# Four small moves in a TensorE-bound encoder layer: places for evacuated tiles, a logarithm in more steps, a later refill, a half-row store

## Chip, core and metric

One core of a Trainium2 chip runs the whole program. The metric is device time in microseconds (us), the median of several executions. TensorE (PE) multiplies, VectorE (DVE) and ScalarE (ACT) work element by element, GpSimd (POOL) does small work beside them, and SyncE (SP) issues the DMA transfers. All five run their own instruction stream in the order in which it was compiled.

## The reference

A hybrid encoder layer with three head groups runs over two request groups of 1024 and 256 rows, with weights in common; the kernel treats their 1280 rows as two halves of 640. All is float32.

```python
def layer(x, mem, ...):
    hn = rms_norm(x, norm_g)
    proj = hn @ w_in                       # 2048 -> xbc, z_ssd, dt, q, k, v, z_att, mq, z_mem
    xbc = silu(centred_dwconv(xbc, ...))
    dt = softplus(dt_raw + dt_bias)
    y = ssd_scan(forward) + ssd_scan(backward) + d_skip * xs      # decay = exp(cumsum(dt * A)), x * dt
    o_ssd = rms_norm(y * silu(z_ssd), ssd_norm_g)
    o_att = window_attention(q, k, v, sink) * silu(z_att)
    o_mem = softmax(mq @ mk.T) @ mv * silu(z_mem)
    return x + concat([o_ssd, o_att, o_mem]) @ w_out
```

## The kernel before

**Products.** Every float32 operand of the large products is split into a high part that TensorE takes in one pass and a low part (the rest), and each product is three matmuls, high by high, low by high, high by low. Weights arrive in pieces of 128x512 (`wraw`, four buffers) and are split by `wsplit` (L214 to L218): ACT copies the high part (`wh`, L216), DVE subtracts for the low part (`wl`, L217). The other operand lies split in SBUF in four quads, `xH0` to `xH3` and `xL0` to `xL3`.

**Blocks.** The program is a list of blocks. `block_tok` (L244) makes 640 rows by 512 columns in five sums (`acc`), one for each 128 rows, over 16 k-steps; the last two k-steps are done tile by tile, so that the five sums end one after the other, and each is evacuated while the next one runs. `block_feat` (L278) is the same with the result turned, and `block_pair` (L1287) makes a product in seven sums instead of eight. The first half's projections come first, then from 493 us on the second half's: kv, z1 of the first half, x0 to x5, kv, q, za, z0, z1, mq, zm, and then the output product o0 to o3 for the first half, and eight `block_pair` units for the second. Blocks follow each other on PE without a gap, and an evacuated tile (`qs` of `ev_raw`, L335; `zs` of `ev_gate`, L315) goes to DRAM from one of two tags, `evt` and `evu`, with two buffers each.

**Beside the blocks.** Everything else (attention, memory attention, the scan) is written as generators in two lanes. `pump` (L158) takes so many steps of each lane for a k-step; a `yield` is where a step ends, and `need` (L169) runs lanes until a given generator is done. A scheduler then orders each engine's stream by its own estimate of the times, so an instruction may be compiled well ahead of or behind its place in the code; on the chip the stream is fixed.

**What the change touches.** `dt_prep` (L568) makes the step sizes for five tiles of 128 rows: a softplus on DVE, `da` (L593), the logarithm's first guess (L596, L597), the sums over rows on PE (`pacs`, L608 to L610, which read `da`, and `lower`, a triangle made on POOL), and two rounds that sharpen the logarithm. A round is an exponential on ACT (L614, `s`) and five operations on DVE (L616 to L620), and the next round's exponential needs the last of them. `refill_o` (L1531) loads the first half's finished heads from DRAM (`oT`) through `chd` (tag `ch`, four buffers) and splits them into a quad; its table says at which k-step which quad is started. `ev_pair` (L1232) adds the seven sums of an output unit into two rows of 640 and stores them. The streams that matter are ACT's, in which a waiting instruction holds the `wh` behind it, and SP's, in which a waiting transfer holds the `wraw` loads behind it.

Of the kernel before, what the change touches and what calls it, by code (L numbers as in the profile page):

```python
# [44 lines left out]
def hymba_encoder_kernel(  # L45
# [80 lines left out]
    def hv(ap, n=8):  # L126
        return ap.rearrange("p (h d) -> p h d", h=n)
# [184 lines left out]
            evac(1, ps[1])  # L312


    def ev_gate(c, base):  # L315
        def f(i, ps):
            z = ev.tile([P, 512], F32, tag="evt" if i % 2 else "evu", name="zs")
            A.activation(z, ps, AF.Tanh, scale=0.5)
            V.scalar_tensor_tensor(out=z, in0=z, scalar=1.0, in1=ps, op0=ALU.add, op1=ALU.mult)
            S.dma_start(z_d[c][base + i], z)  # L320
        return f
# [12 lines left out]

    def ev_raw(dst, base):  # L335
        def f(i, ps):
            if base == 0 and i > 2:
                z = fin.tile([P, 512], F32, tag="tH7" if i == 4 else "tL7", name="qs")
            else:
                z = ev.tile([P, 512], F32, tag="evt" if i % 2 else "evu", name="qs")  # L340
            last_raw[0] = A.activation(z, ps, AF.Copy).ins
            S.dma_start(dst[base + i], z)
        return f
# [224 lines left out]
    def dt_prep(t0):  # L568
        grp = t0 // 5
        ts = slice(t0, t0 + 5)  # L570
        flat = lambda a: a[:, ts, :].rearrange("p t h -> p (t h)")
        t6 = (t0 + 1) % 6
        wj, dd = [a[:, t6:t6 + 5, :].rearrange("p t h -> p (t h)") for a in (wj_all, dd_all)]
        t5 = lambda a: a.rearrange("p (t h) -> p t h", t=5)
        x = flat(dt_all)
        e, s = [mp.tile([P, 512], F32, tag="xs", name=n, bufs=2)[:, :160] for n in "es"]
        w, l = [mp.tile([P, 512], F32, tag=f"ya{i}", name=n, bufs=1)[:, :160] for i, n in enumerate("wl")]
        V.scalar_tensor_tensor(out=e, in0=x, scalar=-1.0, in1=x, op0=ALU.mult, op1=ALU.min)
        A.activation(e, e, AF.Exp)
        V.tensor_scalar(out=s, in0=e, scalar1=2.0, scalar2=None, op0=ALU.add)  # L580
        V.reciprocal(out=s, in_=s)
        V.tensor_mul(s, s, e)
        V.tensor_mul(w, s, s)
        V.tensor_scalar(out=e, in0=w, scalar1=1.0 / 17, scalar2=None, op0=ALU.mult)
        for c in (15, 13, 11, 9, 7, 5, 3):
            V.scalar_tensor_tensor(out=e, in0=e, scalar=1.0 / c, in1=w, op0=ALU.add, op1=ALU.mult)
        V.scalar_tensor_tensor(out=e, in0=e, scalar=1.0, in1=s, op0=ALU.add, op1=ALU.mult)
        V.tensor_scalar(out=e, in0=e, scalar1=2.0, scalar2=None, op0=ALU.mult)
        V.scalar_tensor_tensor(out=x, in0=x, scalar=0.0, in1=e, op0=ALU.max, op1=ALU.add)
        yield  # L590

        da = e
        V.tensor_mul(t5(da), dt_all[:, ts, :], aneg.unsqueeze(1).broadcast_to([P, 5, 32]))  # L593
        yield

        V.tensor_scalar(out=w, in0=x, scalar1=1e-30, scalar2=None, op0=ALU.max)  # L596
        V.tensor_scalar(out=l, in0=w.bitcast(I32), scalar1=math.log(2.0) / 2 ** 23, scalar2=-126.957 * math.log(2.0),  # L597
                        op0=ALU.mult, op1=ALU.add)
        yield
        yield  # L600
        lower = w2("lower")[:, :P]
        G.affine_select(out=lower, in_=ones, compare_op=ALU.is_ge, fill=0.0, base=0,
                        pattern=[[-1, P]], channel_multiplier=1)
        yield
        yield
        ps = psum("pacs")
        p5 = t5(ps[:, :160])
        T.matmul(p5[:, :, 0:16], upper, t5(da)[:, :, 0:16], start=True, stop=True)  # L608
        T.matmul(p5[:, :, 16:32], lower, t5(da)[:, :, 16:32], start=True, stop=True)
        T.matmul(ps[:, 160:320], ones, da, start=True, stop=True)  # L610
        ac = wb("ac", shape=(P, 512))
        A.activation(ac[:, :320], ps[:, :320], AF.Copy)
        for _ in range(2):
            A.activation(s, l, AF.Exp)  # L614
            d = da
            V.tensor_sub(d, w, s)  # L616
            V.tensor_add(s, w, s)
            V.reciprocal(out=s, in_=s)
            V.tensor_mul(d, d, s)
            V.scalar_tensor_tensor(out=l, in0=d, scalar=2.0, in1=l, op0=ALU.mult, op1=ALU.add)  # L620
        A.activation(flat(eacs_all), ac[:, 0:160], AF.Exp)
        A.activation(flat(cd_all), ac[:, 160:320], AF.Exp)
        V.tensor_sub(wj, l, ac[:, 0:160])
        V.tensor_add(dd, wj, ac[:, 160:320])
        A.activation(dd, dd, AF.Exp)
        V.tensor_sub(t5(wj)[:, :, 16:32], t5(wj)[:, :, 16:32], t5(wj)[:, :, 0:16])
        yield
        ps = psum("pact")
        T.transpose(ps[:, :P], ac[:, 0:128], ident)
        T.transpose(ps[:32, P:2 * P], ac[:, 128:160], ident)  # L630
        acT = wb("acT", shape=(P, 512))
        A.activation(acT[:, :P], ps[:, :P], AF.Copy)
        A.activation(acT[:32, P:2 * P], ps[:32, P:2 * P], AF.Copy)
        S.dma_start(ac_d[grp][0:P, :], acT[:, :P])
        S.dma_start(ac_d[grp][P:160, :], acT[:32, P:2 * P])
        yield
# [595 lines left out]
    def ev_pair(u):  # L1232
# [9 lines left out]
        def f(p, ps):  # L1242
            if p == 1:
                A.activation(w[:, 0], ps, AF.Copy)
                add(r0[:, 0], ps, r0[:, 0])
            elif p == 2:
                add(r0[:, 0], ps, r0[:, 0])
            elif p == 6:
                add(w[:, 0], ps, w[:, 0])
            elif p == 5:  # L1250
                add(w[:, 1], ps, w[:, 0])
                add(r0[:, 1], w[:, 1], r0[:, 1])
                add(r1, w, r1)
            elif p == 3:
                add(r0[:, 1], ps, r0[:, 1])
                S.dma_start(hv(y_turned[rows_[0], :], 2), r0)
            elif p == 7:
                add(r1, ps.unsqueeze(1).broadcast_to([P, 2, 320]), r1)
                S.dma_start(y_turned[rows_[1], 320:], r1[:, 1])
            else:  # L1260
                add(r1[:, 0], ps, r1[:, 0])
                S.dma_start(y_turned[rows_[1], :320], r1[:, 0])
# [265 lines left out]
                         gain=vec[:, R_G + 4 * q + j:R_G + 4 * q + j + 1], norm=True) for j in range(4)]  # L1528
        return f

    def refill_o(grp, when):  # L1531
        def f(k):
            if k not in when:
                return []
            q = when[k]
            need((attn, mem_attn, ssd_down, ssd_down)[q], range(grp * 5, grp * 5 + 5))
            return [part(fill_direct, q, j, oT_d[q][grp][:, j, :],
                         gain=None if q < 2 else vec[:, R_SG + 4 * (q - 2) + j:R_SG + 4 * (q - 2) + j + 1])
                    for j in range(4)]
# [171 lines left out]
    queue(0, mem_values, [1])  # L1711
    queue(0, mem_attn, range(8, 10))
    for c in range(2):
        tok("o", w_out_rows(c), ev_out(c * 512), None if c else refill_o(0, {1: 2, 5: 3}), grp=1)
    for c in range(2, 4):
        j0 = 16 * (c - 3)
        for k in block_tok(w_out_rows(c), 5, ev_out(c * 512), before_last=lambda _: beside_step(j0 + 14)):
# [91 lines left out]
```

## Time and profile before

| what | us |
|---|---|
| median of 3 executions (1772.21 to 1774.35) | 1772.34 |
| the profiled execution | 1773.66 |
| its span, first to last instruction | 1772.0 |
| PE busy in it | 1762.2 |
| DVE, ACT, POOL busy | 1246.0, 901.6, 555.6 |

The profile was taken of one execution, whose own time was 1.32 us over the median. Lines of the form "start, length, engine, line, operation, out<-in" are single instructions, or runs of equal ones with their count; what stands in brackets is how long the engine sat idle just before, and which event ended that. The end of a matmul is modelled: a 128x512 one is shown as 0.39 us long, and the next one starts 0.23 us after it. The granted clock of TensorE is a share of its full speed.

### The profile page before, as it was taken

To read this page: it belongs to the slowest core of one execution; us is meant where nothing else is said; L and a number is where in the kernel's file an instruction comes from. 1 tells how busy PE (TensorE), PEld (TensorE's weight loads), DVE (VectorE), ACT (ScalarE), POOL (GpSimd) and SP (SyncE) were. 2 spreads that over 40 slices of the span, in tenths; PEclk is the share of its full clock that TensorE was granted. 3 is DMA by queue.
4 is the path that set the end of the run, shared out by engine and by line. 5 is a ranking of instruction groups with operands and counts; after the bars stand their busy time and mean duration, and the time that the engine had idled before them with its cause. 6 is when DMAs were issued, how large, how long until landed. Compare 5 with 4: busy or idle time off the path is not lost. (4 is left out here: it accounts for less than half of the span.)

```text
span 1772.0 us, 31942 instructions
## 1 busy us (share of the span) xinstructions
PE 1762.2 (99%) x11044; PEld 1608.4 (91%) x11044; DVE 1246.0 (70%) x2351; ACT 901.6 (51%) x2010; POOL 555.6 (31%) x980
## 2 busy tenths in 40 slices
PE   9999999999999999999999999999999999999999
PEld 7889999999998999999889988888988888899999
DVE  5596788888868878878665676566776654766665
ACT  6555455554434756656454555544446533543332
POOL 0105899998810100001001000011110000058775
PEclk9999999999999999999999999999999999999999
DMA  9654444445446645454545645557777755744442
GB/s 308 189 182 130 136 151 146 144 140 169 124 140 209 197 134 151 140 153 122 186 121 173 201 149 161 172 161 249 225 246 226 257 188 148 218 142 148 145 144 77
DMA packets 208210, 301.16 MB, mean 170 GB/s; under 512 B 19568, under 2 KB 86192, under 8 KB 208048
## 3 DMA queue, kind: packets, MB, share of 16 engines
q1 hardware_dynamic: 207904, 299.06, 54.1%
q8 instruction: 87, 1.43, 0.3%
q14 instruction: 75, 0.61, 0.1%
q10 hardware_dynamic: 144, 0.06, 0.0%
HBM read 236.36 MB, written 62.69 MB: 169 GB/s over the span
## 5 line engine op out<-in xcount | busy, mean ns | idle before, releaser
L217 DVE TENSOR_TENSOR wl<-wraw,wh 128x512 fp32r<-128x512 f32 (+1 forms) x480 | 346.4, 724 | 238.4 <-ACT wh L216 225.4
L216 ACT ACTIVATE wh<-wraw 128x512 fp32r<-128x512 f32 (+1 forms) x480 | 292.2, 613 | 301.6 <-PE acc L270 154.6
L268 PE MATMUL acc<-wh,xH 128*128 128x512 f32 (+1 forms) x1088 | 418.1, 385 | 0.0
L270 PE MATMUL acc<-wh,xL 128*128 128x512 f32 (+1 forms) x1088 | 410.4, 377 | 0.0
L269 PE MATMUL acc<-wl,xH 128*128 128x512 f32 (+1 forms) x1088 | 409.5, 376 | 0.0
L270 PEld LDWEIGHTS acc<-wh,xL 128*128 128x128 f32 x1088 | 204.2, 188 | 37.0 <-issue 0.2
L268 PEld LDWEIGHTS acc<-wh,xH 128*128 128x128 f32 x1088 | 204.3, 188 | 36.5 <-issue 2.7
L269 PEld LDWEIGHTS acc<-wl,xH 128*128 128x128 f32 x1088 | 204.5, 188 | 35.0 <-issue 1.2
L303 PE MATMUL acc<-xH,wh 128*128 128x320 f32 x640 | 203.0, 317 | 0.0
L305 PE MATMUL acc<-xH,wl 128*128 128x320 f32 x640 | 198.8, 311 | 0.0
L304 PE MATMUL acc<-xL,wh 128*128 128x320 f32 x640 | 198.5, 310 | 0.0
L216 ACT ACTIVATE sh<-ws 128x384 fp32r<-128x384 f32 x176 | 91.4, 523 | 204.8 <-POOL ws L1284 111.2
L217 DVE TENSOR_TENSOR sl<-ws,sh 128x384 fp32r<-128x384 f32 x176 | 124.4, 710 | 98.3 <-ACT sh L216 96.0
L1284 POOL TENSOR_TENSOR ws<-wraw 128x128 f32<-128x128 f32 x176 | 113.8, 646 | 202.4 <-DMA wraw<-in_w_in_pairs_dram 90.5
L303 PEld LDWEIGHTS acc<-xH,wh 128*128 128x128 f32 x640 | 120.1, 188 | 2.9 <-issue 2.4
L304 PEld LDWEIGHTS acc<-xL,wh 128*128 128x128 f32 x640 | 120.2, 188 | 1.7 <-issue 1.4
L305 PEld LDWEIGHTS acc<-xH,wl 128*128 128x128 f32 x640 | 120.2, 188 | 1.0 <-issue 0.9
L1284 POOL TENSOR_TENSOR ws<-wraw,ws 128x128 f32<-128x128 f32 x176 | 116.5, 662 | 13.8
L1284 POOL TENSOR_TENSOR ws<-ws,wraw 128x128 f32<-128x128 f32 x176 | 118.2, 671 | 0.0
L1284 POOL TENSOR_TENSOR wraw<-wraw 128x128 f32<-128x128 f32 x176 | 111.5, 633 | 13.7
L654 POOL MEMSET lgw<- 128x1 f32 x40 | 4.2, 105 | 312.0 <-DVE lg L718 161.6
L377 DVE SCALAR_TENSOR_TENSOR c<-u,vec,c 128x638 f32<-128x638 f32 (+1 forms) x96 | 90.0, 939 | 1.1 <-ACT c L372 0.4
(442 smaller groups left out, 3931.1 us busy)
## 6 DMA issues: line engine op xcount, KB each, us to landing
wraw<-in_w_in_laid_dram SPq DMA_DIRECT2D x176, 256.0 KB, 2.9
wraw<-in_w_in_pairs_dram SPq DMA_DIRECT2D x112, 256.0 KB, 2.7
wraw<-in_w_out_laid_dram SPq DMA_DIRECT2D x64, 256.0 KB, 3.6
wraw<-in_w_out_pairs_dram SPq DMA_DIRECT2D x64, 256.0 KB, 2.7
rf<-ac SPq DMA_DIRECT2D x40, 256.0 KB, 4.0
rb<-ac SPq DMA_DIRECT2D x40, 256.0 KB, 4.7
wraw<-in_w_mem_laid_dram SPq DMA_DIRECT2D x32, 256.0 KB, 4.3
xst<-in_x_sample_dram SPq DMA_DIRECT2D x20, 256.0 KB, 5.3
```

The source lines that it names most:

```text
L216: a = A.activation(h, raw, AF.Copy)
L217: b = V.tensor_sub(l, raw, h.bitcast(F32))
L268: T.matmul(ps[t][:, :n], sh, h[:, :n], start=(k_ == 0), stop=False)
L269: T.matmul(ps[t][:, :n], sh, l[:, :n], start=False, stop=False)
L270: T.matmul(ps[t][:, :n], sl, h[:, :n], start=False, stop=(k_ == KT - 1))
L303: T.matmul(o, sh, cur["H", q][:, m, c], start=(k == 0), stop=False)
L304: T.matmul(o, sh, cur["L", q][:, m, c], start=False, stop=False)
L305: T.matmul(o, sl, cur["H", q][:, m, c], start=False, stop=(k == KT - 1))
L377: V.scalar_tensor_tensor(out=c[0], in0=u[:, k:k + n], scalar=cw[k], in1=c[0], op0=ALU.mult, op1=ALU.add)
L654: G.memset(w.bitcast(F32)[(slice(None),) + tuple(slice(n - 1, n) for n in shape)], 0.0)
L1284: G.tensor_tensor(out=o, in0=x, in1=y, op=op)
```

## The change

Five edits, none of which changes a product.

1. `out_place` gives the place of an evacuated tile. In the second half's `ev_raw` and `ev_gate` blocks (q, z0, z1, mq; `base` is 5) the last two of the five tiles go to the tag `ch` instead of `evt` and `evu`. Until now `ch` was free in that time, and `refill_o`'s loads took its buffers early.
2. In `dt_prep` the triangle is made two steps earlier, the sums `pacs` come two steps earlier, and there is a step's end after each of the two rounds of the logarithm.
3. `eacs_all` and `cd_all`, two exponentials on ACT, are written ahead of the rounds instead of behind them.
4. `refill_o` in o0 starts quads 2 and 3 at k-steps 2 and 6 instead of 1 and 5. The `need` that drains the lanes stays where it was.
5. `ev_pair` stores the first half of one row as soon as it is complete, and the sum for the other row's first half is made one sum earlier: over the eight units eight stores more, and eight DVE operations more, since one over the full width has become two over half of it.

```diff
+    def out_place(i, base, name):
+        if i > 2 and base == 0 and name == "qs":
+            return fin.tile([P, 512], F32, tag="tH7" if i == 4 else "tL7", name=name)
+        if i > 2 and base:
+            return rp.tile([P, 640], F32, tag="ch", name=name, bufs=CH)[:, :512]
+        return ev.tile([P, 512], F32, tag="evt" if i % 2 else "evu", name=name)
...
-            z = ev.tile([P, 512], F32, tag="evt" if i % 2 else "evu", name="zs")
+            z = out_place(i, base, "zs")
...
-            if base == 0 and i > 2:
-                z = fin.tile([P, 512], F32, tag="tH7" if i == 4 else "tL7", name="qs")
-            else:
-                z = ev.tile([P, 512], F32, tag="evt" if i % 2 else "evu", name="qs")
+            z = out_place(i, base, "qs")
...
         V.tensor_mul(t5(da), dt_all[:, ts, :], aneg.unsqueeze(1).broadcast_to([P, 5, 32]))
+        lower = w2("lower")[:, :P]
+        G.affine_select(out=lower, in_=ones, ...)
         yield
...
-        yield
-        yield
-        lower = w2("lower")[:, :P]
-        G.affine_select(out=lower, in_=ones, ...)
         yield
         yield
         ps = psum("pacs")
...
+        A.activation(flat(eacs_all), ac[:, 0:160], AF.Exp)
+        A.activation(flat(cd_all), ac[:, 160:320], AF.Exp)
         for _ in range(2):
             A.activation(s, l, AF.Exp)
...
-        A.activation(flat(eacs_all), ac[:, 0:160], AF.Exp)
-        A.activation(flat(cd_all), ac[:, 160:320], AF.Exp)
+            yield
...
             elif p == 2:
                 add(r0[:, 0], ps, r0[:, 0])
+                S.dma_start(y_turned[rows_[0], :320], r0[:, 0])
             elif p == 6:
                 add(w[:, 0], ps, w[:, 0])
+                add(r1[:, 0], w[:, 0], r1[:, 0])
             elif p == 5:
                 add(w[:, 1], ps, w[:, 0])
                 add(r0[:, 1], w[:, 1], r0[:, 1])
-                add(r1, w, r1)
+                add(r1[:, 1], w[:, 1], r1[:, 1])
             elif p == 3:
                 add(r0[:, 1], ps, r0[:, 1])
-                S.dma_start(hv(y_turned[rows_[0], :], 2), r0)
+                S.dma_start(y_turned[rows_[0], 320:], r0[:, 1])
...
-    def refill_o(grp, when):
+    def refill_o(grp, when, sooner=0):
         def f(k):
+            if k + sooner in when:
+                need((attn, mem_attn, ssd_down, ssd_down)[when[k + sooner]], range(grp * 5, grp * 5 + 5))
...
-    ... refill_o(0, {1: 2, 5: 3}), grp=1)
+    ... refill_o(0, {2: 2, 6: 3}, sooner=1), grp=1)
```

How the streams move, at three places. Lines of the changed kernel have its own numbers, up to 11 higher.

PE in the second half's q block, before: the end of a k-step's 15 matmuls, the turning of the memory attention's weights (`pmt`) and then the sums of `dt_prep` (`pacs`, which read `da`, here `e`).

```order
L268 MATMUL acc<-wh,xH_6807 128x512
L269 MATMUL acc<-wl,xH_6807 128x512
L270 MATMUL acc<-wh,xL_6808 128x512
L647 MATMUL pmt<-identr,mprw 128x128 x4
L608 MATMUL pacs<-e,upper 128x5x16
L609 MATMUL pacs<-e,lower 128x5x16
L610 MATMUL pacs<-e,one 128x160
```

The same sums in the changed kernel:

```order
L268 MATMUL acc<-wh,xH_6807 128x512
L269 MATMUL acc<-wl,xH_6807 128x512
L611 MATMUL pacs<-e,upper 128x5x16
L612 MATMUL pacs<-e,lower 128x5x16
L613 MATMUL pacs<-e,one 128x160
L270 MATMUL acc<-wh,xL_6808 128x512
```

They now stand behind the second of that k-step's 15 matmuls instead of behind the fifteenth and `pmt`: 13 matmuls and the four of `pmt` earlier. In the first half's `dt_prep` they stand 30 matmuls earlier.

SP at the start of zm, before: the scan's stores and loads (`oT_1`, `cc`, `st`, `yd`, `ydT`) and two loads for o0 and o1 (`yt`).

```order
L1098 DMA cc<-xbc_d 128x2x128
L427 DMA yt<-in_x_sample_dram 128x512 x2
L1114 DMA st_15163<-sb_185 128x512
L1114 DMA st_15171<-sb_185 128x512
L1104 DMA yd<-yp_165 128x512
L1089 DMA oT_1_161<-so 512x1x128
L770 DMA oT_1_155<-oT 512x1x128
L1116 DMA ydT<-yd_175 128x512
```

And in the changed kernel:

```order
L1102 DMA cc<-xbc_d 128x2x128
L188 DMA chd<-oT_0_154 128x640
L1118 DMA st_15163<-sb_185 128x512
L1118 DMA st_15171<-sb_185 128x512
L188 DMA chd<-oT_0_154 128x640 x2
L1093 DMA oT_1_161<-so 512x1x128
L774 DMA oT_1_155<-oT 512x1x128
L1120 DMA ydT<-yd_175 128x512
L1108 DMA yd<-yp_165 128x512
```

Three refill loads of 320 KB, which were issued at 1047 us before, now stand here; the two `yt` loads have moved behind the fourth of them, some 17 transfers later, and one `yd` load stands behind `ydT`.

DVE in o0, before: the refill's low parts (`xL`) and the scan's chain from `xs` to `fl`.

```order
L201 SCALAR_TENSOR_TENSOR xL_16321<-chd,vec,xH_16320 128x640
L217 TENSOR_TENSOR wl<-wraw,wh 128x512
L932 COPY xs<-pxs 128x512
L950 TENSOR_TENSOR xf<-xs,dd_all 128x512
L201 SCALAR_TENSOR_TENSOR xL_16321<-chd,vec,xH_16320 128x640
L960 TENSOR_TENSOR fl<-xf,fh 128x512
```

In the changed kernel `xs` stands ahead of `wl`, and the first `xL` behind `xf`; the four loads of quad 2 stand at the same place in SP's stream as before, only the fourth has one other load ahead of it.

More of the change, by code (lines that the diff above doesn't have):

```diff
@@ L593, in dt_prep @@
         V.tensor_mul(t5(da), dt_all[:, ts, :], aneg.unsqueeze(1).broadcast_to([P, 5, 32]))
+        lower = w2("lower")[:, :P]
+        G.affine_select(out=lower, in_=ones, compare_op=ALU.is_ge, fill=0.0, base=0,
+                        pattern=[[-1, P]], channel_multiplier=1)
         yield
@@ L598, in dt_prep @@
                         op0=ALU.mult, op1=ALU.add)
-        yield
-        yield
-        lower = w2("lower")[:, :P]
-        G.affine_select(out=lower, in_=ones, compare_op=ALU.is_ge, fill=0.0, base=0,
-                        pattern=[[-1, P]], channel_multiplier=1)
         yield
@@ L1535, in f @@
             q = when[k]
-            need((attn, mem_attn, ssd_down, ssd_down)[q], range(grp * 5, grp * 5 + 5))
             return [part(fill_direct, q, j, oT_d[q][grp][:, j, :],
@@ L1713, in hymba_encoder_kernel @@
     for c in range(2):
-        tok("o", w_out_rows(c), ev_out(c * 512), None if c else refill_o(0, {1: 2, 5: 3}), grp=1)
+        tok("o", w_out_rows(c), ev_out(c * 512), None if c else refill_o(0, {2: 2, 6: 3}, sooner=1), grp=1)
     for c in range(2, 4):
```

## Prediction, made before the run

> **What bounds the kernel now.** I read the page's first part, then the waits of PE, then the stages in which they lie.
>
> ```profile
> PE 1762.2 (99%) x11044; PEld 1608.4 (91%) x11044; DVE 1246.0 (70%) x2351; ACT 901.6 (51%) x2010; POOL 555.6 (31%) x980
> ```
>
> PE is busy for 1762.2 of the 1772.0 us of the span. No other engine comes near, so a change can only gain where PE waits, and at the ends of the program. The waits are few:
>
> ```profile
> PE pst L937 <- ACT fh L952: 1.1, 1, 1.1
> PE pmt L647 <- DVE mpr L827: 1.1, 1, 1.1
> PE ppt L647 <- ACT pT L734: 1.0, 1, 1.0
> PE pmo L850 <- ACT mpT L839: 0.8, 1, 0.8
> ```
>
> These four of about 1 us each are what a change can win, 4.0 us together; the other waits are of 0.4 us and less, or the start. The change aims at three of them (`pst` in o0, `ppt` at the start of zm, `pmo` in q) and at the tail. Nothing in it touches `pmt`. The same view shows what a new wait would cost: PE has no slack, so each us in which its next instruction is not ready is a us of the total.
>
> **The change part by part.** A wait counted in a row runs from the modelled end of the matmul before, so it is a lower bound by some 0.2 us; I take the rows.
>
> *Own places.* At the end of mq the last evacuation finds its buffer still being stored:
>
> ```profile
> 1224.83 0.60 ACT L341 ACTIVATE qs<-acc 128x512 f32<-128x512 f32 x1 [0.74 <-PE acc L270]
> 1225.51 0.63 ACT L216 ACTIVATE wh<-wraw 128x512 fp32r<-128x512 f32 x1
> 1227.20 0.60 ACT L341 ACTIVATE qs<-acc 128x512 f32<-128x512 f32 x1 [1.06 <-DMA mq<-qs]
> 1227.69 0.66 ACT L734 ACTIVATE pT<-ppt 128x256 f32<-128x256 f32 x2
> ...
> 1228.12 0.56 PE L647 MATMUL ppt<-identr,lgw 128*128 128x128 f32 x3 [0.95 <-ACT pT L734]
> ```
>
> ACT waits 1.06 us for the store `mq<-qs`, the copy `pT` stands behind it in ACT's stream, and PE's `ppt` waits 0.95 us for `pT`. With a place of its own the evacuation starts when `wh` ends, at 1226.1, and the wait goes: 0.95 us sooner. The evacuations of q, z0 and z1 have no such row with PE behind them, so their new places bring nothing.
>
> What is late next lies 16 us on. PE's `pd` reads `ydT`, which SP issues at 1239.32:
>
> ```profile
> 1233.15 1.01 SPq L427 DMA_DIRECT2D yt<-in_x_sample_dram  x2
> 1239.32 0.66 SPq L1116 DMA_DIRECT2D ydT<-yd  x1
> ...
> 1244.41 0.51 PE L1122 MATMUL pd<-identr,ydT 128*128 128x128 f32 x4
> ```
>
> and in the 24 us around it the queue is full:
>
> ```profile
> q1 hardware_dynamic: 6362, 7.01, 89.7%
> ...
> st<-sb SPq DMA_DIRECT2D x2, 256.0 KB, 6.8
> ydT<-yd SPq DMA_DIRECT2D x2, 256.0 KB, 4.9
> ```
>
> The queue's packets take 89.7% of all 16 engines, loads need up to 6.8 us to land, and 1239.32 + 4.9 is 1244.2: `pd` starts 0.2 us after its load lands. If PE comes 0.95 us sooner it stands there and waits. So the gain is given back unless the load lands sooner too. It has more ahead of it: three `chd` loads of 320 KB (960) instead of two `yt` (512) and one `yd` (256), 192 KB more. The window moved 7.01 MB in 24 us, 0.29 MB a us, so that is 0.66 us later; against it SP issues the loads that hang on PE up to 0.95 us sooner. Bounds: from 0.95 us gained (the queue takes up its 10% of idle time, 1.8 us over 18) to 0.66 us lost. I take 0, since the row of `pd` lies on the landing and the two shifts about cancel.
>
> The Trainium skill (DMA: Bandwidth & Descriptors, Queues, rings and completion order) says that on each DMA engine the entries of a queue are consumed in the order of the ring. By that rule what is issued ahead of `ydT` delays it by its full size, and this edit would lose 0.66 us; the landing of 6.8 us for `st` agrees.
>
> *The logarithm, second half.* Before, the second round's exponential held ACT:
>
> ```profile
> 875.91 0.34 ACT L614 ACTIVATE s<-l 128x160 f32<-128x160 f32 x1 [2.05 <-DVE l L620]
> 876.15 0.61 ACT L216 ACTIVATE wh<-wraw 128x512 fp32r<-128x512 f32 x1
> 876.67 0.58 ACT L839 ACTIVATE mpT<-pmt 128x512 f32<-128x512 f32 x1
> ...
> 877.30 1.16 PE L850 MATMUL pmo<-mpT,mv 128*128 128x128 f32 x8 [0.79 <-ACT mpT L839]
> ```
>
> `s` waits 2.05 us for the first round, `wh` and `mpT` are queued behind it, and `pmo` waits 0.79 us. In the new order the first round runs while ACT does the softmax, and the second `s` is due some 1.5 us sooner. This wait goes: 0.79 us. But `pacs` has moved ahead by 13 matmuls, into the slot of 867.43, and its operand is `da` of L593:
>
> ```profile
> 867.43 0.39 PE L270 MATMUL acc<-wh,xL 128*128 128x512 f32 x1
> ...
> 870.68 0.42 PE L608 MATMUL pacs<-e,upper 128*128 128x80 f32 x2
> ...
> 868.61 0.32 DVE L593 TENSOR_TENSOR e<-dt_all,aneg 128x160 f32<-128x160 f32 x1
> ```
>
> `da` ends at 868.93. DVE's stream up to it is the same in both kernels and runs there without a pause that the rows show, so it comes no sooner. PE, in order, stands before `pacs` from 867.43 to 868.93 with every matmul of the block queued behind: 1.50 us. A price of nothing would need `da` 1.5 us sooner, which nothing in the change does. Bounds 1.3 to 1.8 (0.2 us either way for the way from DVE to PE, by the offset that I named). Together this half is 0.71 us slower.
>
> *The logarithm, first half.* The same, 30 matmuls earlier:
>
> ```profile
> 537.15 0.32 DVE L593 TENSOR_TENSOR e<-dt_all,aneg 128x160 f32<-128x160 f32 x1
> ...
> 537.37 0.39 PE L268 MATMUL acc<-wh,xH 128*128 128x512 f32 x1
> ```
>
> `da` ends at 537.47, the slot is 537.37: 0.10 us lost, bounds 0 to 0.3. The rounds now run between other work; the weights' splits that they push back (`wl`, by up to 4 us) are made two k-steps of 3.4 us ahead (15 matmuls at 0.23), which covers them. If that cover were gone, the wait would be the excess, under 1 us. The triangle on POOL and the two exponentials ahead of the rounds have one answer: no one waits for them, 0.
>
> *The later refill.* SP issues the four loads where it did, so "later" moves only what ACT and DVE do with them:
>
> ```profile
> 1329.87 0.88 DVE L201 SCALAR_TENSOR_TENSOR xL<-chd,vec,xH 128x640 fp32r<-128x640 f32 x1
> 1332.17 0.69 DVE L217 TENSOR_TENSOR wl<-wraw,wh 128x512 fp32r<-128x512 f32 x1 [1.42 <-ACT wh L216]
> 1332.78 0.68 DVE L932 COPY xs<-pxs 128x512 f32<-128x512 f32 x1
> ...
> 1334.10 0.63 ACT L952 ACTIVATE fh<-xf 128x512 fp32r<-128x512 f32 x1 [0.52 <-DVE xf L950]
> ...
> 1334.78 0.50 PE L937 MATMUL pst<-fh,bth 128*128 128x512 f32 x1 [1.09 <-ACT fh L952]
> ```
>
> `xs` now runs in the 1.42 us in which DVE waits, so `xf` starts at 1332.8 instead of 1333.4, and `fh` waits 0.52 us less; 0.09 of that is lost at the next bound, ACT's two `xH` before it. `pst` starts 0.5 us sooner, but the matmul that used to stand between the first `pst` and the one on `fl` now follows it, and `fl` has one `xL` (0.88 us) ahead of it: a wait of some 0.15 us. I take 0.35 us gained, bounds 0 and 0.9. The last pieces of quads 2 and 3 are written some 3 us later, a k-step and more ahead of their use; nobody waits.
>
> *The sooner store.* The tail is what follows the last matmul:
>
> ```profile
> 1768.04 0.31 PE L1318 MATMUL accm<-rH,wl 128*128 128x320 f32 x1
> ...
> 1766.27 1.23 DVE L1240 TENSOR_TENSOR yr<-yu,yr 128x320 f32<-128x320 f32 x2
> 1767.42 0.48 DVE L1240 TENSOR_TENSOR yr<-acc,yr 128x320 f32<-128x320 f32 x1
> 1767.82 1.41 DVE L1240 TENSOR_TENSOR yr<-accm,yr 128x640 f32<-128x640 f32 x2
> ...
> 1769.26 0.33 SPq L1262 DMA_DIRECT2D out_dram<-yr  x1
> ```
>
> The last matmul ends at 1768.35, but DVE is behind: its last addition ends at 1769.23, and the last store leaves at 1769.26. Half of the wide addition at 1766.27 moves into the idle time before it, some 0.3 us off DVE's backlog, so the last store leaves some 0.25 us sooner (bounds 0 and 0.4). In the other seven units the same is hidden by PE; the eight more stores stand where one stood in SP's stream, and take 0.34 us of SP each.
>
> **The sum.** 0 - 0.79 + 1.50 + 0.10 - 0.35 - 0.25 = +0.21 us, 0.2 us slower. The profiled execution took 1773.66 us, 1.32 over the median; no term depends on what lies around the span, so the sum goes on the median: 1772.34 + 0.2 = 1772.5 us. Over 0.2%, 3.5 us, a measurement of this kernel can tell from no change; the three runs alone lie 2.1 us apart.
>
> **The rivals.** *The queue gives way:* `ydT` lands sooner by what PE gains, and the 0.95 us stay. For it speaks the idle tenth of the queue, against it the 6.8 us of `st`. 1772.5 - 0.95 = 1771.6.
>
> *`pacs` does not wait:* `da` is early enough, because DVE gets through sooner or PE comes later. All four gains stand: 0.95 + 0.79 + 0.35 + 0.25 = 2.3 us, 1770.0. Against it speaks that DVE's stream is unchanged up to `da`.
>
> *The refill jams zm,* the case that ends slower: the three `chd` loads come on top, since `yt` and `yd` return before the queue has emptied. `ydT` lands 960 KB later, at 0.29 MB a us 3.3 us, and PE stands at `pd` for 0.95 us more than that, of which it had gained the 0.95: 1772.5 + 3.3 = 1775.8. It decides where `ydT` lands after 1247.7, 3.5 us later than now. For it speaks that the loads moved from 1047 us, where nobody waits for the queue, into its fullest stretch.
>
> ```profile
> 800.00:1000.00 200.00, 198.06 (x1328) 181.13 (x1327) 137.71 (x311) 108.95 (x287) 19.24 (x38) 1.00 0.50 153
> 1200.00:1400.00 200.00, 197.47 (x1234) 170.74 (x1233) 142.02 (x293) 100.61 (x240) 21.88 (x61) 1.00 0.75 239
> ```
>
> The last three columns of these windows are the granted clock, the DMA share and GB/s: waits of 1 us in both leave the clock at 1.00, so a wait costs itself and no more. The Trainium skill (TensorE: Matmul & The Clock Gate, Part 1: The HAM clock gate) says that an idle stretch of some 3.4 us halves the clock until about as long a busy one has passed. By that rule a jam of 3.3 us could cost another 1.7 us, an estimate from that page; no wait here is long enough to show it.
>
> *The edits do nothing that counts:* every wait goes and comes back within its stage, 1772.3.
>
> **How the numbers follow.** My forecast has a chance of 0.5, the queue that gives way 0.2, `pacs` without a wait 0.13, the jam 0.12, nothing at all 0.05. The range takes in the forecast with the bounds of its terms (-2.0 to +1.4 us around 1772.5), the two faster rivals down to 1770.0, and most of the jam: 1769.8 to 1775.3. Faster by over 0.2% means under 1768.8, for which even the four gains would have to reach their upper bounds: 0.04. Slower by over 0.2% means over 1775.9, half of the jam: 0.07. No change that can be told: 0.89.
>
> **What would show it.** In the changed kernel's waits of PE there should be one new row, `pacs` for DVE's `e`, of 1.3 us or more, and none for `pmo`; the evacuation `qs` should have no wait for a DMA, and `ppt` none of 0.95; at `pd` in zm there should be a wait for `ydT`. `pst` should wait about half as long, and the last store leave 0.25 us sooner after the last matmul. I am wrong if `pacs` shows no wait, if zm as a whole takes more than 1 us less or 2 us more, or if PE waits for an operand at a place that I have not named.

## The result and the profile after

The changed kernel takes 1775.9 us (median of 18 executions, 1772.95 to 1780.08), the kernel before in the same runs 1772.64 us (18 executions, 1770.8 to 1775.25): a ratio of 1.0016, interval 1.0009 to 1.0023, so 1.6 to 4.1 us slower. Forecast were 1772.5 us and no change. The profiled execution has a span of 1776.7 us, 4.7 more than that of before, and of PE's waits it shows:

```profile
PE pst L941 <- ACT fh L956: 1.9, 2, 1.5
...
PE pacs L611 <- DVE w L604: 1.0, 1, 1.0
PE pk L559 <- DVE kh L553: 0.7, 1, 0.7
PE pmt L651 <- DVE mpr L831: 0.5, 1, 0.5
...
PE pst L942 <- DVE fl L964: 0.5, 2, 0.2
PE pd L1126 <- DMA ydT<-yd: 0.3, 1, 0.3
```

`ppt` and `pmo` are gone, as the change meant. `pacs` and `pd` are there, as forecast. But `pacs` waits 1.0 us where 1.3 or more was forecast, `pst` waits longer and in two places where half the wait was forecast, and `pk` was in no forecast. To see where the time went I took the start of the first `acc` matmul of each block from both traces; a stage lasts from its block's start to the next one's. The stages that differ by over 0.2 us (first half and second half are the kernel's groups one and two):

| stage | before | after | forecast of the change |
|---|---|---|---|
| z1, first half (526.6 us on) | 60.66 | 64.22 | +0.10 |
| kv, second half | 46.35 | 45.87 | 0 |
| q, second half | 73.63 | 73.87 | +0.71 |
| zm0 | 42.04 | 41.05 | 0 |
| o0 | 73.01 | 75.23 | -0.35 |
| op0 | 24.86 | 25.55 | 0 |
| last matmul's end to the last store's issue | 0.91 | 0.62 | -0.25 |

Two stages make the loss, z1 of the first half and o0. (The 0.7 us of op0 are a wait of one matmul for DVE; the other profiles with the edit of `ev_pair` have 24.70 to 25.02 there. In kv `pmt` waits less; the other profiles, with and without the edits, have 45.5 to 46.3. The first two blocks took 0.50 us more, and the first half's `block_pair` units behind them 0.50 less, so that the two cancel.) In z1 the waits stand close together on PE and ACT; in the profile before, PE sits idle at these places for 0.07 us at most:

```profile
574.63 0.63 ACT L956 ACTIVATE fh<-xf 128x512 fp32r<-128x512 f32 x1 [4.18 <-DVE xf L954]
575.31 0.49 PE L941 MATMUL pst<-fh,bth 128*128 128x512 f32 x1 [0.34 <-ACT fh L956]
576.04 0.50 PE L942 MATMUL pst<-fl,bth 128*128 128x512 f32 x1 [0.23 <-DVE fl L964]
577.64 0.37 PE L559 MATMUL pk<-identr,kh 128*128 128x128 f32 x2 [0.74 <-DVE kh L553]
```

From start to start these three steps take 1.87 us more than the matmuls' own pace. And behind them the granted clock falls. In these windows the columns are length, PE busy and its instructions, granted clock, DMA share, GB/s:

```profile
576.00:578.00 2.00, 1.22 (x7) 1.00 0.00 0
578.00:580.00 2.00, 2.00 (x7) 0.57 0.73 191
580.00:582.00 2.00, 2.00 (x6) 0.58 0.79 233
582.00:584.00 2.00, 2.00 (x10) 1.00 0.93 326
```

At 0.57 and 0.58 for 4 us PE does about 1.7 us less work. So z1 lost 1.9 us to waits and about as much again to the clock. The same stands in o0, where a wait of 1.69 and one of 0.50 us are followed by slices at 0.86 and 0.50; the clock is at one half from 1339.4 to 1342.8 us, again 3.4 us.

**Why z1's waits came.** The rounds of the logarithm now stand on DVE ahead of the operand pieces `xL`. After:

```profile
541.80 1.15 DVE L623 RECIPROCAL s<-s 128x160 f32<-128x160 f32 x1
...
544.00 0.82 DVE L198 TENSOR_TENSOR xL<-chd,xH 128x640 fp32r<-128x640 f32 x1
...
547.28 1.14 DVE L623 RECIPROCAL s<-s 128x160 f32<-128x160 f32 x1
...
550.38 0.81 DVE L198 TENSOR_TENSOR xL<-chd,xH 128x640 fp32r<-128x640 f32 x1
```

Before, the same pieces were through before the first reciprocal:

```profile
542.78 0.82 DVE L198 TENSOR_TENSOR xL<-chd,xH 128x640 fp32r<-128x640 f32 x1
...
544.12 2.29 DVE L198 TENSOR_TENSOR xL<-chd,xH 128x640 fp32r<-128x640 f32 x3
...
548.19 1.15 DVE L618 RECIPROCAL s<-s 128x160 f32<-128x160 f32 x1
```

An `xL` is the last reader of a `chd` buffer, and SP's next load into that buffer waits for it. These loads in SP's stream, before and then after, without the other transfers between them:

```profile
543.63 0.33 SPq L188 DMA_DIRECT2D chd<-in_x_turned_dram  x1
544.97 1.06 SPq L188 DMA_DIRECT2D chd<-in_x_turned_dram  x2
548.09 0.51 SPq L188 DMA_DIRECT2D chd<-in_x_turned_dram  x1
```

```profile
544.85 0.33 SPq L188 DMA_DIRECT2D chd<-in_x_turned_dram  x1
546.42 0.33 SPq L188 DMA_DIRECT2D chd<-in_x_turned_dram  x1
548.83 0.46 SPq L188 DMA_DIRECT2D chd<-in_x_turned_dram  x1
551.23 0.33 SPq L188 DMA_DIRECT2D chd<-in_x_turned_dram  x1
```

The four loads leave 1.2, 1.5, 3.1 and 3.1 us later (the second of the pair at 545.71 before), and the next four later too (the last at 564.43 instead of 562.72). DVE, in order, waits for the landing of these next four with all else behind it:

```profile
566.16 1.75 DVE L194 SCALAR_TENSOR_TENSOR chd<-chd,vec,rbc 128x640 f32<-128x640 f32 x2 [1.81 <-DMA chd<-in_x_turned_dram]
...
570.09 0.89 DVE L194 SCALAR_TENSOR_TENSOR chd<-chd,vec,rbc 128x640 f32<-128x640 f32 x1 [0.58 <-DMA chd<-in_x_turned_dram]
```

These waits are hardly longer than before (1.57 and 0.62 us there); what has moved is the landing that ends them, and with it everything behind. `xf`, 45.4 us after the stage's start before, comes at 47.4 now, and `fh` behind it at 48.1: PE had come to `pst` at that time.

Which delay counts, the other traces tell. From the stage's start to `xf` DVE is busy for 45.2 to 45.8 us with and without the edit of the logarithm (two kernels with other work put into z1 left out here). Its idle time, without the waits for landing, is 3.3 us in each of the eleven profiles without the edit and 4.5 in each of the three with it. The waits for landing are 2.4 us in the mean in both (1.6 to 3.4). So the new loss is 1.2 us of other idle time. Its new waits are these, while an earlier one, for POOL, got 0.5 us shorter. After:

```profile
556.82 0.29 DVE L546 TENSOR_TENSOR kr<-kr,krr 128x128 f32<-128x128 f32 x1 [0.87 <-POOL krr L124]
...
558.49 0.49 DVE L553 TENSOR_TENSOR kh<-kr,kh 128x128 fp32r<-128x128 f32 x2 [0.38 <-ACT kh L551]
559.32 0.82 DVE L198 TENSOR_TENSOR xL<-chd,xH 128x640 fp32r<-128x640 f32 x1 [0.34 <-ACT xH L197]
```

Before, operations of the second round (`e`, `l`) stood between the same steps, and DVE waited 0.12 us there:

```profile
556.05 0.28 DVE L541 TENSOR_TENSOR kr<-kr,krr 128x128 f32<-128x128 f32 x1
556.25 0.32 DVE L620 SCALAR_TENSOR_TENSOR l<-e,l 128x160 f32<-128x160 f32 x1
...
557.28 0.28 DVE L548 TENSOR_TENSOR kh<-kr,kh 128x128 fp32r<-128x128 f32 x1
...
558.04 0.83 DVE L198 TENSOR_TENSOR xL<-chd,xH 128x640 fp32r<-128x640 f32 x1
```

The rounds had filled the time in which POOL makes `krr` and ACT makes `kh`; done earlier, they leave DVE idle there. The `xL` behind comes 1.4 us later after the stage's start, the second four loads wait for it (the last leaves at 37.9 us in the mean of the three, 36.5 in the eleven), and `xf` comes at 47.2 us in the mean (46.6 to 47.6) against 45.7 (44.9 to 46.8). That the first four loads leave late costs little: one wait of 0.37 us for landing in the change, and none of that length in the two other kernels.

PE follows. Where it waits at `pk` for 0.27 us or more, `pk` starts 3.7 to 3.8 us after `xf` in every profile, whatever happens at `pst`, and the stage ends 15.2 to 15.6 us after `xf` in 14 of the 16 profiles; in the two others the clock was lower in it. This was so before the change: `pk` waits 0.7 us or more also in four kernels that have the old logarithm and no other edit in z1.

**Why o0's wait grew.** SP's loads for quad 2 and the end of the chain on ACT and PE, after:

```profile
1327.24 1.27 SPq L188 DMA_DIRECT2D chd<-oT  x3
1328.56 0.43 SPq L926 DMA_DIRECT2D rb<-ac  x1
1329.03 0.43 SPq L188 DMA_DIRECT2D chd<-oT  x1
...
1336.00 0.83 ACT L200 ACTIVATE xH<-chd,vec 128x640 fp32r<-128x640 f32 x1 [1.12 <-DMA chd<-oT]
1336.74 0.61 ACT L956 ACTIVATE fh<-xf 128x512 fp32r<-128x512 f32 x1
1337.40 0.50 PE L941 MATMUL pst<-fh,bth 128*128 128x512 f32 x1 [1.54 <-ACT fh L956]
```

`xf` was sooner, as forecast. But a load `rb` now stands ahead of the fourth load, that piece lands late, ACT waits 1.12 us for it, and `fh` is the next instruction in ACT's stream. The text ahead of the prediction had named that one other load.

### The profile page after: what moved, and what is told of

The parts are those of the page before. It is cut to its first block, busy times and chain, and to the rows that moved or that the text cites. A ratio compares the mean times of both kernels' runs of the same rounds, so it can differ in the third digit from the quotient of the medians.

```text
span 1776.7 us, 31951 instructions
## 1 busy us (share of the span) xinstructions
PE 1766.1 (99%) x11044; PEld 1610.3 (91%) x11044; DVE 1249.3 (70%) x2359; ACT 902.2 (51%) x2010; POOL 556.1 (31%) x980
## 4 chain that ended last, share of the span: by engine, by line
PE 94%; DMA 2%; DVE 2%; issue 1%; ACT 0%; SPq 0%; POOL 0%; DVEq 0%; ACTq 0%
PE acc L268 12%; PE acc L270 12%; PE acc L269 12%; PE acc L1324 7%; PE acc L1322 7%; PE acc L1323 7%; PE acc L303 5%; PE acc L305 5%; PE acc L304 5%; PE accm L1322 3%; PE accm L1323 3%; PE accm L1324 3%; PE po L748 1%; PE py L1018 1%; PE ppt L651 1%; PE pmo L854 1%
```

## The experiments

Each kernel was timed in five rounds beside the kernel before (three of them, far off, gave only four or five executions). A stage's length is from the one profiled execution of each kernel, and those differ by up to 1.5 us for the same code; so I lean on lengths where several kernels share the code.

**1. The parts of the change.** Theory R: the logarithm in z1 of the first half. Theory L: the moved loads in zm and o0. The first kernel is the change without edits 2 and 3, so with `dt_prep` as before; the second has these two alone. The core of the first, against the change:

```diff
+        yield
+        yield
         ps = psum("pacs")
...
-        A.activation(flat(eacs_all), ac[:, 0:160], AF.Exp)
-        A.activation(flat(cd_all), ac[:, 160:320], AF.Exp)
         for _ in range(2):
...
-            yield
+        A.activation(flat(eacs_all), ac[:, 0:160], AF.Exp)
+        A.activation(flat(cd_all), ac[:, 160:320], AF.Exp)
```

> The change without its edit of the logarithm (own places, later refill and sooner store stay). Theory R (the rounds of group one, made sooner, put DVE behind in the stage z1 of group one, so that the buffers of the operand pieces come free later, their loads land later in a full queue and PE waits there): about 1.0 us faster than before, 1771.4 to 1772.0, and no wait of PE at the first chunk sums of z1. Theory L (the loads that the own places and the refill moved cost the time, in the stages zm and o0): 1774.5 or more, with a wait of about 2 us at the chunk sums of o0.

Measured: 1772.77 us, ratio 1.0000 (0.9992 to 1.0009), z1 61.56 with `pk` waiting 0.75 us and `pst` of z1 not at all, o0 73.79 with `pst` waiting 1.7 us. The time fits neither theory.

> The kernel before with the edit of the logarithm alone, both groups. Theory R: 2.0 us (the waits alone) to 3.6 us (with a lower granted clock behind them) slower in group one, some 0.2 us slower in group two: 1774.7 to 1776.3. Theory L, and the prediction's sum for this edit: 0.8 us slower, 1773.3.

Measured: 1774.27 us, 1.0013 (1.0005 to 1.0022), between the two forecasts; z1 61.81, within what the old logarithm shows elsewhere, and q 74.18.

The next two take the halves apart (`dt_first` is called for tile 0, `dt_second` for tile 5):

```diff
+    def dt_prep(t0):
+        return dt_second(t0) if t0 else dt_first(t0)
```

> The change with the old logarithm for group one and the new one for group two. Theory R: 1771.5 to 1772.3, the granted clock 1.00 in the stage z1 of group one, and PE waiting for the operand of the running sums in group two by 1.0 us as in the change. Theory L: as the change, 1775 and more.

Measured: 1774.23 us, 1.0012 (1.0003 to 1.0021), z1 60.42, `pacs` waiting 0.8 us. A miss for R.

> The kernel before with the new logarithm for group one alone. Theory R: 2.0 to 3.6 us slower, 1774.6 to 1776.2, with waits of PE for the chunk sums and the key transposes of z1 (about 2 us together) and a granted clock under 1.00 behind them. Theory L: 1772.7 (the prediction's 0.10 us for this half).

Measured: 1774.28 us, 1.0013 (1.0004 to 1.0021), z1 62.85, and the waits that R names, `pst` for `fl` 0.50 and `pk` 0.88 us from start to start; the time is a little under R's range, and the clock stayed at 1.00 in this profile.

Neither theory holds alone. The first half costs 1.0013 by itself, far from the forecast 0.10 us; but without it the change is still slower than before, and without the logarithm it is level although two edits should gain. So there are more losses: the second half of the logarithm, and something among the other three edits. What the second half costs can't be told from these times: the new logarithm in both halves took 1774.27 us, in the first alone 1774.28, with some 1.5 us of uncertainty either way.

**2. The other edits.** The later refill alone:

```diff
-        tok("o", w_out_rows(c), ev_out(c * 512), None if c else refill_o(0, {1: 2, 5: 3}), grp=1)
+        tok("o", w_out_rows(c), ev_out(c * 512), None if c else refill_o(0, {2: 2, 6: 3}, sooner=1), grp=1)
```

> The kernel before with the later refill alone. Theory A (the copy fh stands in ACT's stream behind an operand piece whose load lands late, so PE waits longer for it at the chunk sums of o0): 0.7 to 1.6 us slower, 1773.2 to 1774.0, the stage o0 73.2 us or more long against 71.9 to 73.0 without the edit. The prediction's term: 0.35 us faster, 1772.1, o0 about 72.5.

Measured: 1773.4 us, 1.0005 (0.9997 to 1.0014), o0 73.94, `pst` waiting 1.8 us. The time alone can't tell; the stage and the wait are those of theory A.

Own places and sooner store alone (edits 1 and 5), tried twice:

> The kernel before with the own places and the sooner store alone (no edit of the logarithm, the refill where it was). Theory A, by which the loss of the refill hid a gain of these two in the run without the logarithm: 0.6 us from the places and 0.3 from the tail, 1771.5, with no wait of PE for pT at the start of zm. The prediction's terms (the places nothing, the store 0.25): 1772.2, with a wait at pd that gives the gain back.

> The kernel before with the own places and the sooner store alone, a second time, since the first time left its gain at the edge of what is measured. Theory (0.4 us from the places, 0.3 us from the tail, both by the profiles so far): 0.7 us faster than before, within 0.9990 and 0.9999. Rival (the first result was chance): 1.0000 or over.

Measured: 1771.17 us, 0.9993 (0.9984 to 1.0002), and 1771.53 us, 0.9994 (0.9985 to 1.0003), with zm0 at 41.05 and 41.10 and the last store 0.62 us after the last matmul. Each interval just takes in 1; two results on the same side make the gain likely, of about 1 us.

The later refill with its fourth load in its old place in SP's stream, the pieces still made later:

```diff
+            def pair():
+                g2, g3 = fill(2), fill(3)
+                kept.append(g3)
+                next(g2)
+                next(g3)
...
+            if sooner:
+                return [part(fill, 0), part(fill, 1), pair, fourth]
```

> The kernel before with the later refill alone, but the fourth piece's load is issued right behind the third's, ahead of SP's load rb, as in the kernel before; its operand pieces are made where the later refill makes them. Theory A4 (the fourth load, put behind a load rb of 256 KB, lands late, and fh stands behind its piece in ACT's stream): the fourth piece is written by 21.3 us after the start of o0 instead of 21.8 to 22.5, fh starts by 22.4 instead of 22.5 to 23.2, the stage o0 takes 72.0 to 72.9 us and the kernel 1772.0 to 1772.6. Rival A0 (the later refill costs by its place in ACT's and DVE's streams, wherever the load is): o0 73.2 us or more, 1773.4 as the later refill alone.

Measured: 1771.41 us, 0.9996 (0.9987 to 1.0005), o0 71.61, and `fh` 20.85 us after the start of o0. In this kernel's trace the four loads leave together, the fourth piece follows the third without a wait, and `fh` comes behind it:

```profile
1323.31 1.74 SPq L188 DMA_DIRECT2D chd<-oT  x4
1325.10 1.12 SPq L922 DMA_DIRECT2D rb<-ac  x2
...
1330.10 1.54 ACT L200 ACTIVATE xH<-chd,vec 128x640 fp32r<-128x640 f32 x2
1331.56 0.63 ACT L952 ACTIVATE fh<-xf 128x512 fp32r<-128x512 f32 x1
```

A4 holds, and A0 falls; stage and time even came out below A4's ranges. Up to `fh`, ACT's and DVE's streams have the same order as with the later refill alone, so the place of one load between two others is what makes the later refill a loss.

**3. Is it DVE's delay in z1?** Three more reciprocals on DVE at that place, with the old logarithm:

```diff
+        if t0 == 0:
+            for _ in range(3):
+                V.reciprocal(out=s, in_=s)
```

> The kernel before with the old logarithm and three more reciprocals of 1.15 us on DVE in group one (their result is not used), ahead of the operand pieces of the stage z1: DVE is put behind by about 1.5 to 2.5 us there, with no other edit. Theory R: SP's loads of the next pieces leave 1 to 2 us later, xf and fh come 1 us or more later, the stage takes 62.0 us or more against 60.4 to 61.6, and the kernel 1773.4 to 1775. Rival P (the sums and exponentials that come sooner, not DVE's delay, disturb the stage): 1772.4, the stage as before.

Measured: 1774.23 us, 1.0010 (1.0001 to 1.0019). The first four loads leave late, as in the change: 18.2, 20.2, 20.9 and 25.2 us after the stage's start, where it was 18.3, 19.9, 22.3 and 24.7 in the change and 17.0 to 21.5 before. The stage took 61.56 us, under the 62.0 expected, with `pk` waiting 0.8 us and `pst` not at all: `xf` came only 0.85 us later than before, and 0.5 us after the mean of the kernels without any edit there, not 1.4. DVE's waits for landing shrank to 1.2 us, which took up part of its extra work. So a delay of DVE is shown to hold back these loads, but their lateness alone does not cost what z1 lost; that fits the idle time at `kr` and `kh` as the larger part, which no kernel tested by itself. The time is slower by just more than its interval, while the profiled z1 lies within what the kernels without an edit there have (60.42 to 61.96).

The other way round, the rounds on POOL in place of DVE:

```diff
-            V.reciprocal(out=s, in_=s)
+            G.tensor_mul(s, s, s)
+            G.tensor_tensor(out=s, in0=s, in1=mhalf[:, :1].broadcast_to([P, 160]), op=ALU.pow)
```

> The kernel before with the new logarithm for group one, whose two rounds run on POOL instead of DVE (the quotient by a power of the square), so that DVE is not put behind. Theory R: 1771.8 to 1772.8, the stage z1 of group one 60.4 to 61.6 us long as with the old order, and SP's loads of operand pieces there leave as in the kernel before. Rival P (not the rounds on DVE but the sums and exponentials that come sooner disturb this stage): as with the new logarithm for group one alone, 1774.3, z1 61.8 us or more.

Measured: 1831.54 us, 1.0329 (1.0315 to 1.0343). The power alone took 52 us, and DVE stood behind it with the weights' splits in its stream, so this run decides nothing between R and P, and P had no other test.

**4. What a wait costs.** Waits put into PE's stream at four quiet places, a chain from PE over DVE and back; `hold(6)` and `hold(1)`:

```diff
+    def hold(n):
+        with tc.issue_after(last_mm[0].ins):
+            T.matmul(psum("hold")[:, :80], ones, ht, start=True, stop=True)
+        ps = psum_last[0]
+        V.tensor_copy(ht, ps[:, :80])
+        for _ in range(n - 1):
+            V.tensor_add(ht, ht, ht)
+        held[:] = [T.matmul(psum("hold")[:, :80], ones, ht, start=True, stop=True).ins]
```

> The kernel before with four waits put into PE's stream, in the stages z0, z1 and mq of group two and in o1: a small product, six small operations of DVE on it, a second small product, and all further products of the block behind it; each holds PE for some 1.5 to 2.5 us. Theory C (the granted clock falls after a wait of this length, and takes about as much again): 1782 to 1788, with slices of a clock under 1.00 behind the waits and a mean clock under 0.9995 in most runs. Rival N (the lower clock comes by chance and not from waits): 8 us slower and no more, 1780, with a lower clock in as few runs as the kernel before has (4 of 35).

> As the kernel with four long waits, with one small operation of DVE instead of six in each, so that PE is held for some 0.7 to 2.0 us. Theory C (a wait must fill most of a stretch of about 3.4 us before the clock falls): each wait costs its own length plus 0.8 us for the two products, no slice behind a wait under 1.5 us shows a clock under 1.00, and the kernel takes 1777 to 1782. Rival (any wait of over 1 us halves the clock behind it): 1.7 us more for each, 1784 or more.

Measured, the long ones: 1799.12 us, 1.0146 (1.0130 to 1.0161); the short ones: 1778.1 us, 1.0041 (1.0027 to 1.0055). The long waits came out longer than meant, 3.6, 3.5, 5.4 and 3.0 us from start to start, and their stages grew by 6.9, 5.6, 8.1 and 6.3 us against the profile before: 2.1 to 3.3 us more than each wait. The windows of the third and behind it, and those of the short kernel's longest wait of 1.7 us, with columns as above:

```profile
1194.90:1200.40 5.50, 0.31 (x2) 0.84 0.51 143
1200.40:1202.00 1.60, 1.57 (x5) 0.50 0.00 0
...
1204.00:1206.00 2.00, 2.00 (x7) 0.63 0.00 0
1206.00:1208.00 2.00, 2.00 (x10) 1.00 0.04 8
```

```profile
1030.50:1032.40 1.90, 0.35 (x4) 1.00 0.48 138
1032.40:1034.40 2.00, 2.00 (x10) 1.00 0.00 0
```

At each of the four long waits the clock falls to one half, for 3.4 us once and for 6.8 us three times, in part while PE still waits; in the profile the short waits of 0.5 to 1.7 us leave it at 1.00, and their stages grew by 1.0 to 2.7 us, each wait and 0.3 to 1.0 us for its products. The long kernel took more time than either theory had said, since its waits were longer than they were to be, so theory C is not tried at the length it was meant for; that long waits bring the clock down and short single ones don't is shown. One of the short kernel's five executions had a mean clock under 1.00.

**5. Do the gains stand together?** The change with the old logarithm and the fourth load in place; then the same with the new logarithm for the second half, whose `pacs` comes one lane step later:

```diff
         yield
         yield
+        yield
         ps = psum("pacs")
```

> The change with the old logarithm in both groups, and with the fourth load of each refill issued right behind the third's: own places, sooner store, and the later refill without its fault. If the gains stand together: 0.4 (places) + 0.3 (tail) + 0.9 (o0 at 71.6) = 1.6 us faster than before, 1770.8, ratio about 0.9991. If they are given back at a next bound: 1771.6 to 1772.4, with a wait of PE at a place in zm or o0 that the kernels with one part do not have.

> As the kernel with three gains, with the new logarithm for group two, but one lane step more ahead of the running sums, so that they stand 11 instructions later in PE's stream than in the change. Theory S (the loss of the new order in group two is PE's wait for the operand of the sums): no wait at the sums, the stage q of group two 72.6 to 73.1 us against 73.7 to 74.2 with the new order, and the kernel as the one with three gains. Rival (the new order costs by what DVE and ACT do in it): 73.7 us or more, 0.9 us slower than the kernel with three gains.

Measured: 1771.55 us, 0.9993 (0.9984 to 1.0002), zm0 41.36, o0 72.35; and 1772.13 us, 0.9996 (0.9988 to 1.0005), q 73.40, o0 72.43. The first has a wait of 0.7 us at `pd` for `ydT`, so there the gain of the places is partly given back, as the prediction had it. The second has no wait of 0.2 us or more at `pacs`, but q lies between the mean lengths with the old and the new order, above the 72.6 to 73.1 of theory S and below the 73.7 of the rival. It has a wait of 0.5 us at `pmo`, which the new order was to remove, and the next stage shows a wait at `pk`. So the wait for the sums is likely a part of the second half's loss; that it is all of it isn't settled. Neither version beats the kernel before beyond its interval.

## Why the prediction was wrong, point by point

All profiles together give each term a size. Counted are the stages of the kernels that share the code there, 13 to 16 profiles for a stage:

| term | without the edit | with it | measured | forecast |
|---|---|---|---|---|
| logarithm, first half (z1) | 61.04 (11 profiles, 60.42 to 61.96) | 62.96 (3, 61.81 to 64.22) | +1.9 | +0.10 |
| logarithm, second half (q) | 73.14 (12, 72.78 to 73.90) | 73.92 (3, 73.70 to 74.18) | +0.8 | +0.71 |
| own places (zm0) | 41.46 (9, 41.07 to 42.04) | 41.12 (7, 41.04 to 41.36) | -0.3 | 0 |
| later refill (o0) | 72.54 (9, 71.85 to 73.08) | 74.05 (4, 73.22 to 75.23) | +1.5 | -0.35 |
| sooner store (tail) | 0.91 | 0.62 | -0.3 | -0.25 |

The sum is 3.6 us, and the medians differ by 3.3. Such a close fit is in part luck: three of the terms rest on three or four profiles, and the profile of the change, which has a lower clock for 3.4 us both in z1 and in o0, counts in them. Without it z1 lost 1.3 us and o0 1.1.

- *The logarithm, first half: wrong.* The step that failed is "the weights' splits that they push back (`wl`, by up to 4 us) are made two k-steps of 3.4 us ahead (15 matmuls at 0.23), which covers them". That cover holds for `wl`: in z1 of the change no `acc` matmul waits for one. But the prediction asked only what the rounds push back, and of that only `wl`. It put at nothing what the rounds leave behind: 1.2 us in which DVE now waits for POOL and ACT, ahead of an `xL`. Behind an `xL` stands a buffer, behind the buffer a load on SP, and behind its landing DVE itself; so `xf` came 1.4 us later, and PE, with `pk` 3.7 us behind `xf`, stood for it. That the edit costs time is shown by the runs; the path is read from the traces. The 0.10 us for `pacs` came out as 0.24 us at most (a wait of 0.23 and 0.24 in two profiles with the new order, none in the change).
- *The later refill: wrong.* "SP issues the four loads where it did" is what failed: the fourth went behind `rb`. The rest of the term was right, and where the load is put back o0 takes 72.1 us in the mean of three profiles (71.61 to 72.43), 0.4 us less than with the early refill, against 0.35 forecast.
- *The logarithm, second half: right in its net, by luck in part.* `pacs` stands and waits for `da`, and starts when `da` ends (871.46 us):

```profile
870.20 0.40 PE L269 MATMUL acc<-wl,xH 128*128 128x512 f32 x1
871.61 0.42 PE L611 MATMUL pacs<-e,upper 128*128 128x80 f32 x2 [1.01 <-DVE w L604]
...
871.14 0.32 DVE L598 TENSOR_TENSOR e<-dt_all,aneg 128x160 f32<-128x160 f32 x1
```

  From start to start PE stood 1.18 us where 1.50 was forecast, since DVE came to `da` half a microsecond sooner against PE than in the profile before. But the 0.79 us of `pmo` that this was set against are one draw: of the twelve profiles with the old order six have no such wait of 0.2 us or more, and one has 1.1; their mean is 0.27. The waits at `pacs` of the three with the new order are 0.80, 1.01 and 1.29 us, 1.03 in the mean. So both terms were too large by about half a us, and the two errors cancel: 1.03 - 0.27 = 0.76, near the 1.50 - 0.79 = 0.71 of the forecast.
- *Own places: the mechanism right, its size a little off.* The evacuation starts when `wh` ends, and `pd` waits for `ydT`; the trace after has both:

```profile
1228.65 0.63 ACT L216 ACTIVATE wh<-wraw 128x512 fp32r<-128x512 f32 x1
1229.34 0.60 ACT L346 ACTIVATE qs<-acc 128x512 f32<-128x512 f32 x1
...
1246.98 0.52 PE L1126 MATMUL pd<-identr,ydT 128*128 128x128 f32 x4 [0.34 <-DMA ydT<-yd]
```

  In that execution zm0 kept all of its 1.0 us, the rival "the queue gives way"; over all profiles 0.3 us are kept. The wait of 0.95 us at `ppt` was itself larger than in the others: of the nine profiles without the edit four have none of 0.2 us or more and four have 0.25 to 0.69, and the mean is 0.35.
- *Sooner store: right.* The last store leaves 0.62 to 0.63 us after the last matmul's end in all seven kernels that have the edit, against 0.91 in all nine without.
- *A wait costs itself and no more: wrong in general.* It was read from waits of about 1 us, and for single ones it holds. For two or three waits close together it doesn't always. The profiled execution of the change lost about 1.7 us to the clock at 578 us and as much at 1339. Half of the change's 18 executions have a mean granted clock under 1.00 and a median of 1777.53 us; the other half have 1773.98. Of the kernel before that are 10 of 104 executions. Without a lower clock the change is thus 1.3 us over the 1772.64 us of before, and with one 4.9. One stretch of 3.4 us at one half takes 1.7 us and brings the mean to 0.999, which is what seven of the nine show (the two others 0.998). So these executions must have lost something over 1 us elsewhere too, and over all 18 the clock makes an estimated 1.0 us in the mean; how the rest is shared out isn't settled.
- *The sum's bounds.* The upper bounds of the terms add up to 1.76 us over the forecast, and not to the "+1.4" that the prediction gives; with the right sum its range stays the same.

The Trainium skill (TensorE: Matmul & The Clock Gate, Part 1: The HAM clock gate) says that the clock goes to one half after an idle window of some 3.4 us and comes back after a busy one, and that the windows run free of what the kernel does. The runs agree as to the half and the time (0.50 for 3.4 or 6.8 us), and that the Trainium skill calls the effect run-variable fits what was seen: waits of 1.87 us within 3.1 us, and of 2.19 within 2.5, were followed by the lower clock in the change, while waits of 1.87 and 0.50 us at the same place of o0, in the kernel without the logarithm, did not. A wholly idle window was not needed for it here: about 2 us of waiting within some 3 us was at times enough.

The prediction had said that it would be wrong "if PE waits for an operand at a place that I have not named", and `pk` and `pst` of z1 are that place. None of the four rivals came true as a whole; the slower one, the jam in zm, did not occur (zm0 took 41.05 us). That its time of 1775.8 us lies next to the 1775.9 measured is chance.

## What to carry to other kernels

When an instruction is moved ahead of others on an engine, ask what it filled at its old place: the engine may now wait there. Follow what is put back not only to the next reader but to the buffers that those instructions free, the loads that wait for these buffers, and the engine that waits for the loads; and compare the whole order of SP's stream, since one transfer that slips between four others can undo a gain. A wait of 1 us in one profiled execution is one draw: before it is counted as gain, see whether other executions of the same code have it. Comparing the idle time of one engine by its causes over many traces shows which wait is new. Where PE is the bound, waits that fall close together can cost more than their sum, because the clock can follow.

## What the runs showed of the hardware that was not expected

- Waits of PE that fill over half of about 3 us can be followed by half the granted clock for 3.4 us (578.3 to 581.7 us and 1339.4 to 1342.8 in the change); waits of 3.0 to 5.4 us were so all four times, for 3.4 or 6.8 us, and their stages grew by 2.1 to 3.3 us beyond the wait.
- A power on POOL over 128x160 took 26 us in the kernel with the rounds on POOL, where a product or a difference of the same shape took 0.5.
- The first two blocks of the program (`mk` and `mv`) together take 88.3 to 89.4 us in the 16 profiles, a spread of 1.1 us at a place that no edit touches.
